# Loading A through casting DMAs from GpSimd, straight into the transposes' input

One Trainium2 chip, one core. The metric is the device time of the kernel in microseconds (us), the median of several executions; all compared runs are in the fast state, with a mean granted TensorE clock of 0.98 to 1.00 of full speed. A profiled execution's span is some 2 us shorter than its time.

## The reference

```python
# a: 4096 x 4096 float32, b: 4096 x 4096 float32, alpha: 0.01
x = np.matmul(a, b)
return np.where(x > 0, x, alpha * x)
```

## The kernel before

The product runs in bf16: 8192 matmuls of 128x128 weights by 512 columns. The output is cut into **regions** of 512 rows by 1024 columns, eight PSUM banks each; a region takes four steps over k (`u`), 1024 deep each, the first one split in two. Two regions that follow each other (h = 0, 1) use the same 1024 columns of B. TensorE needs A transposed: each 128-row block is loaded as fp32 in four DMAs, each of which puts a quarter of the columns on 32 partitions; DVE (in the start for h = 1, ACT) casts it to bf16, and DVE's 32x32 block transpose then leaves k on the partitions.

```python
subs = [(0, 0, 4, 0), (0, 4, 4, 512)] + [(u, 0, 8, 1024 * u) for u in range(1, KU)]
at_pool = ...tile_pool(name="at", bufs=HALVES * KU)
bt_pool = ...tile_pool(name="bt", bufs=KU + 2)
a32_pool = ...tile_pool(name="a32", bufs=4)
a16_pool = ...tile_pool(name="a16", bufs=2)
b32_pool = ...tile_pool(name="b32", bufs=4)
o_pool = ...tile_pool(name="oo", bufs=2)
# ... cut

def load_a(mb, h, sub, mt, scalar=False):
    u, c0, kc, k0 = sub
    # ... cut: allocate at[mb, h, u]
    row = ((mb * HALVES + h) * MT + mt) * P
    w = 32 * kc
    a32 = a32_pool.tile([P, 4, w], FP32, name="a32")
    for q in range(4):
        src = a[row:row + P, k0 + q * w:k0 + (q + 1) * w]
        nc.sync.dma_start(a32[32 * q:32 * q + 32], src.rearrange("(g i) w -> i g w", i=32))
    a16 = a16_pool.tile([P, 4, kc, 32], BF16, name="a16")
    a32_v = a32.rearrange("p g (j c) -> p g c j", c=kc)
    if scalar:
        nc.scalar.copy(a16, a32_v)
    else:
        nc.vector.tensor_copy(a16, a32_v)
    dst = at[mb, h, u][:, c0:c0 + kc, mt * P:(mt + 1) * P]
    nc.vector.transpose(dst.rearrange("p c (g i) -> p g c i", g=4), a16)

def load_b(pi, n, sub, c, scalar=False):
    # ... cut: allocate bt[pi, u]
    b32 = b32_pool.tile([P, RN], FP32, name="b32")
    src = b[k0:k0 + kc * P, n * RN:(n + 1) * RN].rearrange("(p c) n -> p c n", c=kc)
    nc.sync.dma_start(b32, src[:, c, :])
    # ... cut: cast to bt on ACT (start) or DVE

# the first two regions; `ahead` emits the loads of the next step
elif last:                                  # last step of a region
    for mt in range(MT):
        for c in range(kc):
            go(mt, c)                       # matmuls of row block mt
        spill(mt)                           # activation, then
                                            # nc.gpsimd.dma_start(place(0, h, ...), o)
        ahead(mt)
```

SP, GpSimd and the others each work off their instructions in the order in which the program emits them, so what an engine issues waits for everything emitted earlier on that engine (GpSimd's timeline under the result shows it: an output at 97.65 us, one at 101.10, and only then the next loads, at 101.99).

## Time and profile before

| | before |
|---|---|
| time, first rounds | 1837.36 us (1833.26 to 1838.29) |
| matmul time at full pace | 8192 x 0.2158 = 1768 us |
| end of region 0 | 113.4 us |
| PE's waits in the first 135 us | 45 us, of which 35 before 92 us |
| DMA, 8 to 60 us | 268 GB/s at share 1.02 |

1768 us is what TensorE needs with every operand at hand, so the question is only what the first two regions lose. The end of region 0 is read from the timeline of ACT: the activation of its last row block starts when the last matmul of that block is done. In this line (start, duration, group, idle time before it) that is at 113.44 us.

```profile
113.44 1.09 ACT L237 ACTIVATE o<-ps 128x512 f32<-128x512 f32 x2 [1.37 <-PE ps L106]
```

In the profile PE is TensorE, PEld its weight load, DVE VectorE, ACT ScalarE, POOL GpSimd and SP SyncE; what follows "<-" in brackets ended an engine's wait. The lines for all this are in the prediction; two more are needed for later: the windows view of the stage with loads of both A and B (columns: PE, weight load, DVE, ACT, POOL busy with counts, granted clock, DMA share, GB/s), and the page's line on the chain that ended last.

```profile
8.00:60.00 52.00, 30.31 (x105) 11.40 (x107) 20.93 (x24) 16.74 (x16) 0.00 (x0) 0.74 1.02 268
```

```profile
PE ps L106 93%; DMA b<-in_b_dram 4%; DMA a<-in_a_dram 1%; SPq L82 0%; ACT bt L101 0%; ACT a L86 0%; DVE at L90 0%; ACT o L294 0%; SPq L99 0%; ACT o L237 0%; ACTq L86 0%; ACTq L237 0%
```

Where packet times are quoted, they are means of the trace's packet records by queue and size. When a part of A or B "had started" is read from the same records, on the clock of the views (the first packet of the load queue is at 1.75 to 1.77 us in every run). The recorded expectations have such times 1 to 2 us later, as they were set by the last packet of each run.

The record of a packet holds the bytes written. A packet of a casting DMA writes half of what it reads, so in the GB/s and KB of the views below A counts half wherever a DMA casts. I say "read" where I have put it at its full size.

### The profile page before, as it was taken

Reading aid. Unit: us, or ns where it says so; the run is one execution under the profiler, and the core shown is the slowest. Engines: PE = TensorE matmul, PEld = TensorE weight load, DVE = VectorE, ACT = ScalarE, POOL = GpSimd, SP = SyncE. Lnnn points to the kernel's source line nnn. Section 1 sums busy time; section 2 is a strip of 40 time slices with the busy share of each in tenths; the row PEclk is TensorE's granted clock in tenths of the full one; section 3 lists DMA queues with packets and bytes.
Section 4 is the critical chain, followed back from the end, with each engine's and each line's share of the span. In section 5 each row is a group of like instructions: output and inputs, shape, how many; then the busy total and the mean of one; then the engine's idle time right before and its main releaser. Section 6 shows DMA issues by size and latency. Waiting matters only on the chain.

```text
span 1834.5 us, 19653 instructions
## 1 busy us (share of the span) xinstructions
PE 1777.4 (97%) x8041; PEld 804.5 (44%) x8204; DVE 536.0 (29%) x685; ACT 207.0 (11%) x310; POOL 73.3 (4%) x128
## 2 busy tenths in 40 slices
PE   5679999999999999999999999999999999999999
PEld 1234444444444444444444444444444444444444
DVE  3434431127642203023661311202665130311000
ACT  3363000000000000000000000000000000000001
POOL 0000000000000000000000000000000000000000
PEclk7889999999999999999999999999999999999999
DMA  9989975338765718254684734716678281644111
GB/s 249 268 218 302 364 274 205 138 128 214 195 243 192 267 57 329 97 186 132 183 259 180 262 152 172 287 46 212 161 188 307 115 337 58 233 180 153 77 46 47
DMA packets 171163, 353.67 MB, mean 193 GB/s; under 512 B 19008, under 2 KB 100928, under 8 KB 171072
## 3 DMA queue, kind: packets, MB, share of 16 engines
q1 hardware_dynamic: 153216, 287.38, 49.3%
q0 software_dynamic: 17856, 65.02, 9.0%
q8 instruction: 64, 1.05, 0.2%
q14 instruction: 27, 0.22, 0.0%
HBM read 285.21 MB, written 67.11 MB: 192 GB/s over the span
## 4 chain that ended last, share of the span: by engine, by line
PE 93%; DMA 5%; ACT 1%; issue 1%; SPq 0%; DVE 0%; ACTq 0%
PE ps L106 93%; DMA b<-in_b_dram 4%; DMA a<-in_a_dram 1%; SPq L82 0%; ACT bt L101 0%; ACT a L86 0%; DVE at L90 0%; ACT o L294 0%; SPq L99 0%; ACT o L237 0%; ACTq L86 0%; ACTq L237 0%
## 5 line engine op out<-in xcount | busy, mean ns | idle before, releaser
L106 PE MATMUL ps<-bt,at 128*128 128x512 bf16 x8029 | 1772.9, 381 | 51.2 <-DVE at L90 29.6
L106 PEld LDWEIGHTS <-at 128*128 128x128 bf16 x8192 | 803.0, 98 | 1021.1 <-DVE at L90 35.2
L103 DVE CAST bt<-b 128x1024 bf16<-128x1024 f32 x384 | 256.9, 692 | 876.1 <-PE ps L106 575.3
L294 ACT ACTIVATE o<-ps 128x512 f32<-128x512 f32 x240 | 130.7, 595 | 1524.5 <-PE ps L106 1386.7
L90 DVE STREAM_TRANSPOSE at<-a 128x1024 bf16<-128x1024 bf16 (+1 forms) x160 | 165.1, 1032 | 218.3 <-PE ps L106 141.4
L88 DVE CAST a<-a 128x1024 bf16<-128x1024 f32 (+1 forms) x140 | 122.2, 873 | 70.8 <-DMA a<-in_a_dram 70.8
L298 POOL DMA_DIRECT2D out_dram<-o x116 | 68.2, 588 | 1531.8 <-ACT o L294 1526.3
L101 ACT CAST bt<-b 128x1024 bf16<-128x1024 f32 x32 | 33.5, 1046 | 64.8 <-DMA b<-in_b_dram 64.8
L86 ACT CAST a<-a 128x1024 bf16<-128x1024 f32 (+1 forms) x20 | 33.1, 1673 | 19.8 <-DMA a<-in_a_dram 19.7
L238 POOL DMA_DIRECT2D out_dram<-o x8 | 4.9, 608 | 172.1 <-ACT o L237 172.1
L237 ACT ACTIVATE o<-ps 128x512 f32<-128x512 f32 x16 | 8.7, 597 | 14.7 <-PE ps L106 8.9
L131 PE MATMUL ps<-w 128*128 128x512 bf16 x12 | 4.4, 548 | 2.3 <-ACT w L128 2.3
L131 PEld LDWEIGHTS <-w 128*128 128x128 bf16 x12 | 1.5, 133 | 4.7 <-ACT w L128 2.3
L128 ACT ACT_TABLE_LOAD x1 | 1.3, 1283 | 0.7 <-PEq L316 0.7
L127 DVE MEMSET w<- 128x256 uint32 x1 | 0.3, 272 | 0.9 <-PEq L316 0.9
L128 ACT ACTIVATE w<-w 128x8 bf16<-128x8 bf16 x1 | 0.2, 210 | 0.0
L316 POOL MEMSET const-float32-0.0<- 128x1 f32 x1 | 0.1, 99 | 0.2 <-issue 0.2
L316 POOL MEMSET const-bfloat16-1.0<- 128x1 bf16 x1 | 0.1, 103 | 0.0
L316 POOL MEMSET const-float32-1.0<- 128x1 f32 x1 | 0.1, 99 | 0.0
L316 POOL MEMSET const-uint8-127<- 128x1 uint8 x1 | 0.1, 99 | 0.0
## 6 DMA issues: line engine op xcount, KB each, us to landing
b<-in_b_dram SPq DMA_DIRECT2D x416, 512.0 KB, 5.5
out_dram<-o POOLq DMA_DIRECT2D x124, 512.0 KB, 3.4
a<-in_a_dram SPq DMA_DIRECT2D x384, 128.0 KB, 4.4
a<-in_a_dram SPq DMA_DIRECT2D x256, 64.0 KB, 2.3
out_dram<-o SPq DMA_DIRECT2D x8, 256.0 KB, 2.0
```

Of the source, the lines that this page charges most:

```text
L86: nc.scalar.copy(a16, a32_v)
L88: nc.vector.tensor_copy(a16, a32_v)
L90: nc.vector.transpose(dst.rearrange("p c (g i) -> p g c i", g=4), a16)
L101: nc.scalar.copy(bt[pi, u][:, c0 + c, :], b32)
L103: nc.vector.tensor_copy(bt[pi, u][:, c0 + c, :], b32)
L106: nc.tensor.matmul(ps, at[mb, h, u][:, c, mt * P:(mt + 1) * P], bt[pi, u][:, c, nt * NT:(nt + 1) * NT], start=first, stop=last,)
L128: nc.scalar.activation(w[:, :8], w[:, :8], LRELU, alpha=alpha)
L131: nc.tensor.matmul(wp, w[:, :P], w, start=True, stop=True)
L237: nc.scalar.activation(o[:, nt * NT:(nt + 1) * NT], done, LRELU, alpha=alpha)
L238: nc.gpsimd.dma_start(place(0, h, pairs[0], mt), o)
L294: nc.scalar.activation(o[:, cols], banks[mt, nt], LRELU, alpha=alpha)
L298: nc.gpsimd.dma_start(to, o)
```

## The change

The intent is to let the DMA do the cast: fp32 in HBM is rounded to bf16 on the way into the transposes' input. That removes one pass of DVE or ACT over A, its fp32 buffers, and most of what SP issues in the start. Such DMAs are issued by GpSimd. Two row blocks are taken per load, so most transposes have 2048 elements a partition (1024 in the first step), and they read with the stride, in elements, that the cast had before.

```diff
-    a32_pool = ctx.enter_context(tc.tile_pool(name="a32", bufs=4))
-    a16_pool = ctx.enter_context(tc.tile_pool(name="a16", bufs=2))
+    a16_pool = ctx.enter_context(tc.tile_pool(name="a16", bufs=4))
...
-        row = ((mb * HALVES + h) * MT + mt) * P
+        row = (mb * HALVES + h) * RM + 2 * mp * P
         w = 32 * kc
-        a32 = a32_pool.tile([P, 4, w], FP32, name="a32")
+        a16 = a16_pool.tile([P, 8, w], BF16, name="a16")
         for q in range(4):
-            src = a[row:row + P, k0 + q * w:k0 + (q + 1) * w]
-            nc.sync.dma_start(a32[32 * q:32 * q + 32], src.rearrange("(g i) w -> i g w", i=32))
-        a16 = a16_pool.tile([P, 4, kc, 32], BF16, name="a16")
-        a32_v = a32.rearrange("p g (j c) -> p g c j", c=kc)
-        if scalar:
-            nc.scalar.copy(a16, a32_v)
-        else:
-            nc.vector.tensor_copy(a16, a32_v)
-        dst = at[mb, h, u][:, c0:c0 + kc, mt * P:(mt + 1) * P]
-        nc.vector.transpose(dst.rearrange("p c (g i) -> p g c i", g=4), a16)
+            src = a[row:row + 2 * P, k0 + q * w:k0 + (q + 1) * w]
+            nc.gpsimd.dma_start(a16[32 * q:32 * q + 32], src.rearrange("(g i) w -> i g w", i=32))
+        dst = at[mb, h, u][:, c0:c0 + kc, 2 * mp * P:2 * (mp + 1) * P]
+        nc.vector.transpose(
+            dst.rearrange("p c (g i) -> p g c i", g=8), a16.rearrange("p g (j c) -> p g c j", c=kc)
+        )
```

Cut: the loops that call `load_a` count pairs of row blocks (`mp`) in place of `mt`, the interleaving of A and B loads is adapted ("abbabb", "abbbabbbbb"), and the first step's matmuls go by pairs of row blocks.

More of the change, by code (lines that the diff above doesn't have):

```diff
@@ L70, with load_a @@
     bt = {}
-    def load_a(mb, h, sub, mt, scalar=False):
+    def load_a(mb, h, sub, mp):
         u, c0, kc, k0 = sub
@@ L159 @@
                 pieces = [
-                    lambda mb=mb, h=h, sub=sub, mt=mt: load_a(mb, h, sub, mt)
+                    lambda mb=mb, h=h, sub=sub, mp=mp: load_a(mb, h, sub, mp)
                     for sub in subs_of[u]
-                    for mt in range(MT)
+                    for mp in range(MT // 2)
                 ]
@@ L182, in step_loads @@
         if h:
-            return [lambda mt=mt: load_a(0, 1, sub, mt, True) for mt in range(MT)]
-        order = "abababab" if sub[2] == 4 else "ababbabbabbb"
+            return [lambda mp=mp: load_a(0, 1, sub, mp) for mp in range(MT // 2)]
+        order = "abbabb" if sub[2] == 4 else "abbbabbbbb"
         made, na, nb = [], 0, 0
@@ L187, in step_loads @@
             if what == "a":
-                made.append(lambda mt=na: load_a(0, 0, sub, mt))
+                made.append(lambda mp=na: load_a(0, 0, sub, mp))
                 na += 1
@@ L245 @@
         if i == 0:
-            for c in range(kc):
-                for mt in range(c):
-                    go(mt, c)
-                for cc in range(c + 1):
-                    go(c, cc)
+            for mts, cs in (((0, 1), (0, 1)), ((2, 3), (0, 1)), ((0, 1, 2, 3), (2, 3))):
+                for c in cs:
+                    for mt in mts:
+                        go(mt, c)
             for quarter in range(4):
```

## The prediction

> **What bounds the kernel now.** I read the page first: busy times, then the 40 slices.
>
> ```profile
> span 1834.5 us, 19653 instructions
> PE 1777.4 (97%) x8041; PEld 804.5 (44%) x8204; DVE 536.0 (29%) x685; ACT 207.0 (11%) x310; POOL 73.3 (4%) x128
> ...
> PE   5679999999999999999999999999999999999999
> ...
> PEclk7889999999999999999999999999999999999999
> ```
>
> PE is full in all slices but the first three (a slice is 45.9 us), and so is its clock. In the chain of work that ended last, 49 matmuls take 10.74 us and the next such piece starts 10.79 to 10.80 us later, 50 matmuls with the one between: 0.216 us each. The product needs 8192 of them, 8192 x 0.216 = 1768 us. So about 66 us of the 1834 are not matmul time, and only those can be won. The waits of PE over the whole run and after 100 us say where they lie:
>
> ```profile
> PE ps L106 <- DVE at L90: 29.6, 10, 5.6
> PE ps L106 <- ACT bt L101: 12.9, 8, 3.1
> ```
>
> ```profile
> PE ps L106 <- DVE at L90: 4.0, 3, 1.6
> PE ps L106 <- ACT bt L101: 0.4, 1, 0.4
> ```
>
> Columns: microseconds in total, times, longest. After 100 us PE waits 4.4 us in all; its last wait ends at 133 us. The rest is start. From then on PE is the bound, and nothing that DVE, ACT or the DMAs save there can shorten the run. The start is two regions: region 0 (rows 0 to 511 by the first 1024 columns of B, 256 matmuls, 55 us at full pace) ends at about 113 us; region 1 (the next 512 rows, same B) follows. What holds region 0 is seen in the windows view (PE time, granted clock, DMA share, GB/s), and in what ended the engines' idle time between 8 and 100 us:
>
> ```profile
> 8.00:100.00 92.00, 54.76 (x202) 21.39 (x206) 0.78 1.00 264
> 100.00:113.00 13.00, 12.52 (x49) 5.15 (x49) 0.82 0.59 184
> 123.00:135.00 12.00, 9.46 (x44) 4.00 (x43) 1.00 1.07 231
> 200.00:229.00 29.00, 28.84 (x133) 13.11 (x135) 1.00 0.98 359
> ```
>
> ```profile
> ACT bt L101 <- DMA b<-in_b_dram: 60.2, 31, 4.6
> DVE a L88 <- DMA a<-in_a_dram: 54.1, 19, 5.4
> ```
>
> Both casting engines wait for transfers, and the DMA engines are at share 1.00 for 92 us. **The start is bound by DMA throughput**, at only 264 GB/s, while the same engines move 359 GB/s at the same share from 200 to 229 us, where only B and some output move. The packets of A are what is slow. Averaging the trace's packet records by size: a 4 KB packet (B) has a median of 159 ns where A is absent and a mean of 219 ns from 8 to 100 us; a 1 KB packet of A has a tenth percentile of 46 ns and a mean of 73 ns there; a 512-byte packet of A, median 27 and mean 34 ns.
>
> **What the Trainium skill says.** (1) "SBUF — State Buffer", Door 1: The DMA port swizzle: the rate into SBUF depends on how many of 16 ports the partitions reach, 27 GB/s each ("DMA: Bandwidth & Descriptors", Specifications, for the rate per engine), and 32 adjacent partitions reach 8. Every DMA of A goes to 32 partitions. Two engines on one port have 13.6 GB/s each, so 1024 bytes need an estimated 75 ns; the mean of 73 against the fastest 46 agrees. (2) "DMA: Bandwidth & Descriptors", SWDGE vs HWDGE vs iDMA: a cast in a DMA is possible only from GpSimd, whose cores write each descriptor. The trace before has GpSimd issue output DMAs of 128 packets, 0.59 us each. Nothing casts in a DMA there, and no page I found states the rate of a casting packet. (3) "SBUF — State Buffer", the "DVE blocks DMA" trap: VectorE in a two-port mode keeps GpSimd from writing descriptors. In the start VectorE would only transpose, at 1245 ns for 1024 elements, no fast mode, so I expect no such stall there; later its B casts (692 ns for 1024, faster than one element a cycle) could each delay a DMA of A by 0.7 us, against a lead of seven slots of 13.8 us (64 matmuls each).
>
> **The change, part by part.**
>
> ```profile
> L88 DVE CAST a<-a 128x1024 bf16<-128x1024 f32 (+1 forms) x140 | 122.2, 873 | 70.8 <-DMA a<-in_a_dram 70.8
> L86 ACT CAST a<-a 128x1024 bf16<-128x1024 f32 (+1 forms) x20 | 33.1, 1673 | 19.8 <-DMA a<-in_a_dram 19.7
> L298 POOL DMA_DIRECT2D out_dram<-o x116 | 68.2, 588 | 1531.8 <-ACT o L294 1526.3
> ```
>
> Removed: 140 DVE casts (122 us) and 20 ACT casts (33 us). DVE is busy 29% and PE-bound stages do not feel it; of these only the latency in the start counts. 160 transposes become 80 of twice the size: from 711 ns for 512 and 1245 for 1024 elements the slope is 1.04 ns an element, so 2.31 us for 2048. The strided side moves from the cast to the transpose; the cast ran one element a cycle with it (1058 ns for 1024), so I charge nothing. Removed from SP: 640 issues of about 0.4 us. SP was not the main bound.
>
> Added on GpSimd: 320 DMAs of 256 packets. From 0.53 to 0.59 us for 128 packets I estimate 1.1 us each, 4.4 us for a tile of 256 rows. The 40 DMAs of region 0 need 44 us, less than their transfer stage, so generation is not the bound there. The first tile comes at about 0.7 + 4.4 + 2 (landing, as the small DMAs before), transpose 1.25: first matmul at 8.4 us, against 7.94 before. No gain, no loss.
>
> **Transfers in region 0.** HBM bytes stay the same, 8.4 MB of A and 16.8 MB of B; packets too: 4096 of 512 B, 6144 of 1 KB, 4096 of 4 KB. But A writes half the bytes into the half-reached ports. If casting is free, an engine's share of a port now carries 512 bytes in 38 ns, less than the 46 ns of the fastest packet, so the read side sets 46 (27 for the small) and B is stretched less, say 170 ns. Over 16 engines: A 4096 x 27/16 = 6.9 us and 6144 x 46/16 = 17.7; B 4096 x 170/16 = 43.5; sum 68 us, with a start of 3 us done at 71. Before: last B tile on hand near 99.5. Then comes what came before too: the last step runs rows outermost, 64 matmuls = 13.8 us, so region 0 ends near 85 instead of 113. **Gain 28 us.**
>
> **Order on GpSimd, given back.** Loads of region 1's A stood on SP, which ran ahead (they begin at 93 us). On GpSimd they stand behind region 0's output DMAs, which wait for PE. In program order the first tile of region 1 follows the output of row block 1, the second that of row block 3, thus after region 0's last matmul. With T that end: output at T+2, generation until T+6.5, landing T+8.5, transpose T+9.8. The first step of region 1 needs all four row blocks in its first quarter, so PE idles about 9 us; the next two steps each need two more tiles of 4.4 us generation against 6.9 us of matmuls, some 2 to 3 us more each. About 14 us instead of 4: **loss 10 us.** By region 2 the queue is ahead: GpSimd needs 44 us for region 1's A, PE 55 us. In later row blocks the same order costs nothing, by the seven-slot lead. B for region 2 (16.8 MB) now need not queue on SP behind A, but still waits for buffers.
>
> Sum with free casting: 1837 - 28 + 10 = 1819 us.
>
> **Rivals.** *The port story is wrong or casting costs about what it saves* (1 KB packet near 73 ns, B near 219): the transfer stage stays, the loss on GpSimd's order stays: 1837 + 8 to 10 = 1846. For: rows of A lie 16 KB apart, and the slow mean could be HBM's; against: the 46 and 73 ns pair fits two engines to a port. *Casting packets are slow* (an estimate for the case: 150 ns for 1 KB, 75 for 512 B): A in region 0 takes 6144 x 150/16 + 4096 x 75/16 = 77 us, with B at 170 a stage of 120; region 0 ends near 137, region 1 is fed at 77 us against 55 of matmuls: 24 + 20 to 30 slower, 1880 to 1890. Nothing in the profile speaks for or against, since no DMA here casts. *GpSimd becomes the bound* (2 us and more per DMA): region 0 takes 80 us of generation, region 1 as much against 55 us of matmuls; gain gone, 1845 to 1865. Against: 0.53 us for 128 packets. *All hidden:* after 135 us PE is full whatever happens; this holds for 1700 us of the run and is why every outcome but the slow packet stays within 2%.
>
> **Range and chances.** 2% is 37 us. Faster than 1800 needs more than half of the 66 us; even pure B rate (25.2 MB at 415 GB/s, the best slices of the stretch from 135 to 229 us, is 61 us) with no loss of order only just gets there: 0.06. Slower than 1874 needs packets over about 130 ns or generation over 2.5 us: 0.13. The rest, 0.81, is the same within 2%. I weigh free casting about 0.55, the equal case 0.2, slow packets or slow GpSimd 0.25. Point 1822 us, range 1804 to 1868.
>
> **What would show it.** Right: region 0 ends at 80 to 90 us, the rate from 8 us to there is above 320 GB/s, 1 KB packets have a mean near 46 to 50 ns and B's falls towards 170; PE's waits put 8 to 10 us on the transpose at the start of region 1, released by a DMA that GpSimd issued after region 0's last output; DVE falls by about 130 us without effect; matmuls after 150 us still come every 0.216 us. Wrong: packets of the software queue above 100 ns, GpSimd instructions above 1.5 us each, VectorE waiting on A throughout region 1, or any PE wait after region 2 begins, which would mean that the seven-slot lead does not cover output DMAs ahead of loads.

## The result

The changed kernel took 1827.97 us (1827.43 to 1828.4, 4 runs), the kernel before 1837.82 us in the same rounds (1833.26 to 1842.58). The ratio is 0.9946, 95% interval 0.992 to 0.9971. Here and below a ratio is the mean time of one kernel's fast runs over that of the other's of the same rounds, so not quite the ratio of the quoted medians. The gain is real and half a per cent: the same within 2%, and inside the predicted range. The kernel before scatters more than the changed ones and moved between 1834 and 1839 us from one set of rounds to another, so each ratio is to the kernel before in the same rounds. The changed kernel itself ran in the first rounds only: what is said of a few microseconds between it and the experiments compares different rounds, and how far the changed kernels move from one set to another was not measured.

The page after, busy times and the groups that changed (busy us, mean ns, then idle time before them):

```profile
span 1825.7 us, 18868 instructions
...
PE 1776.4 (97%) x8041; PEld 804.5 (44%) x8204; DVE 475.6 (26%) x465; ACT 174.3 (10%) x290; POOL 253.6 (14%) x448
...
PE ps L101 93%; DMA a<-in_a_dram 4%; POOL a L81 0%; POOL out_dram L233 0%; DVE at L83 0%; ACT o L288 0%; DVEq L83 0%; POOLq L81 0%; POOLq L233 0%; POOLq L310 0%
...
L83 DVE STREAM_TRANSPOSE at<-a 128x2048 bf16<-128x2048 bf16 (+1 forms) x80 | 219.4, 2779 | 365.1 <-DMA a<-in_a_dram 241.9
...
L81 POOL DMA_DIRECT2D a<-in_a_dram x320 | 183.4, 587 | 83.4 <-DMA a<-in_a_dram 50.5
```

All casts of A are gone, yet DVE's total fell by only 60 us: the transposes now take 219 us, not 165. In the chain that ended last, 4% of the span moved from B's transfers to A's. The windows view for the two stages that matter, and PE's waits after 100 us:

```profile
8.00:60.00 52.00, 27.60 (x80) 9.83 (x82) 12.61 (x6) 30.03 (x29) 15.47 (x27) 0.67 1.18 340
60.00:100.00 40.00, 37.92 (x172) 16.96 (x174) 15.34 (x5) 4.58 (x8) 6.87 (x12) 1.00 0.58 128
100.00:120.00 20.00, 12.77 (x51) 5.36 (x53) 8.66 (x6) 0.80 (x2) 16.51 (x29) 0.83 1.07 141
```

```profile
PE ps L101 <- DVE at L83: 7.3, 2, 6.1
```

From 8 to 60 us the DMAs moved 340 GB/s in place of 268. In bytes read it is more: the casting queue, q0, wrote 2.51 MB in these 52 us and so read twice as much, which makes 388 GB/s. But PE did less in that stage, 27.60 us in place of 30.31, and from 60 to 100 us it was nearly full (37.92 of 40) while the DMAs were half idle. The timelines of PE and of ACT say how:

```profile
43.42 1.89 PE L101 MATMUL ps<-bt,at 128*128 128x512 bf16 x4 [3.90 <-DVE at L83]
54.50 16.70 PE L101 MATMUL ps<-bt,at 128*128 128x512 bf16 x63 [9.20 <-DVE at L83]
72.91 26.94 PE L101 MATMUL ps<-bt,at 128*128 128x512 bf16 x121 [1.71 <-DVE at L83]
101.05 1.04 PE L101 MATMUL ps<-bt,at 128*128 128x512 bf16 x4 [1.20 <-DVE at L83]
108.22 112.13 PE L101 MATMUL ps<-bt,at 128*128 128x512 bf16 x501 [6.13 <-DVE at L83]
```

```profile
99.72 1.09 ACT L232 ACTIVATE o<-ps 128x512 f32<-128x512 f32 x2 [2.36 <-PE ps L101]
```

Region 0 ends at 99.7 us, 13.7 us earlier than before. PE lies still until 54.5 us for the second tile of step u = 1. Then, at the border to region 1, it waits 1.20 + 6.13 us. What it waits for in the first case is told by the DMA view for 8 to 60 us (packets, MB and share of the engines of the casting queue; then size written and median us from issue to landing), and by the waits of GpSimd up to 100 us (us in total, times, longest):

```profile
q0 software_dynamic: 7203, 2.51, 40.6%
...
b<-in_b_dram SPq DMA_DIRECT2D x29, 512.0 KB, 6.0
a<-in_a_dram POOLq DMA_DIRECT2D x19, 128.0 KB, 19.7
```

```profile
POOL a L81 <- DMA a<-in_a_dram: 45.3, 24, 2.9
```

A casting DMA of 256 packets took 19.7 us to land, while a DMA of B, with twice the bytes to read, took 6.0. By the packet records B's 16.8 MB had started to the last packet at 59 us, but only half of A's 8.4 MB at 50 us. GpSimd had eight loads in flight at most, in this kernel and in all the others that load A from it, and before 100 us it waited 45.3 us for one to land before it issued the next; whether that number comes from the chip or from the software is not shown. In the second case it is the order on GpSimd, seen in the timeline of POOL:

```profile
97.65 0.56 POOL L233 DMA_DIRECT2D out_dram<-o  x1 [0.64 <-ACT o L232]
101.10 0.55 POOL L233 DMA_DIRECT2D out_dram<-o  x1 [2.88 <-ACT o L232]
101.99 7.99 POOL L81 DMA_DIRECT2D a<-in_a_dram  x14 [0.35 <-issue]
```

The second A tile of region 1 is issued after region 0's last output.

So there were four things to test: whether the transfer rate rose because half the bytes go to the half-reached ports; whether A was late because B's queue took the engines' time; whether the order on GpSimd cost what it seems to; and what the slow transposes cost.

### The profile page after: what moved, and what is told of

Same layout as the page of the kernel before. It is cut to its first block, busy times and chain, and to the rows that moved or that the text cites. A ratio compares the mean times of both kernels' runs of the same rounds, so it can differ in the third digit from the quotient of the medians.

```text
span 1825.7 us, 18868 instructions
## 1 busy us (share of the span) xinstructions
PE 1776.4 (97%) x8041; PEld 804.5 (44%) x8204; DVE 475.6 (26%) x465; ACT 174.3 (10%) x290; POOL 253.6 (14%) x448
## 4 chain that ended last, share of the span: by engine, by line
PE 93%; DMA 4%; issue 2%; POOL 1%; DVE 0%; ACT 0%; POOLq 0%; DVEq 0%
PE ps L101 93%; DMA a<-in_a_dram 4%; POOL a L81 0%; POOL out_dram L233 0%; DVE at L83 0%; ACT o L288 0%; DVEq L83 0%; POOLq L81 0%; POOLq L233 0%; POOLq L310 0%
## 5 line engine op out<-in xcount | busy, mean ns | idle before, releaser
L83 DVE STREAM_TRANSPOSE at<-a 128x2048 bf16<-128x2048 bf16 (+1 forms) x80 | 219.4, 2779 | 365.1 <-DMA a<-in_a_dram 241.9
L81 POOL DMA_DIRECT2D a<-in_a_dram x320 | 183.4, 587 | 83.4 <-DMA a<-in_a_dram 50.5
```

The lines of the kernel that those rows point to most:

```text
L81: nc.gpsimd.dma_start(a16[32 * q:32 * q + 32], src.rearrange("(g i) w -> i g w", i=32))
```

## The experiments

Ten kernels ran, in three sets.

### Region 0's outputs from SP

```diff
-                nc.gpsimd.dma_start(place(0, h, pairs[0], mt), o)
+                (nc.gpsimd if h else nc.sync).dma_start(place(0, h, pairs[0], mt), o)
```

> Changed kernel, with the four output DMAs of region 0 issued by SP, so that region 1's loads of A no longer stand behind them on GpSimd. Theory (order on GpSimd costs time at the start of region 1): PE's waits after 100 us fall from 7.3 us to under 2, the loads of region 1's A are issued before 85 us, and the time falls from 1828 by 6 to 8 us, to 1820 to 1822. Rival (those waits come from transfer or transpose, not from the order): PE still waits 5 us or more there, time within 2 us of 1828.

Measured: 1818.17 us (1817.68 to 1819.74), ratio to before 0.9906. After 98 us PE has no wait left at all. The timelines of PE and of POOL:

```profile
55.31 164.91 PE L101 MATMUL ps<-bt,at 128*128 128x512 bf16 x750 [10.89 <-DVE at L83]
```

```profile
61.82 4.75 POOL L81 DMA_DIRECT2D a<-in_a_dram  x8 [1.59 <-DMA a<-in_a_dram]
```

PE's matmuls run on from 55.31 us without a gap over the border, and GpSimd goes straight on to region 1's A from about 62 us. The mechanism is shown. The gain is 9.8 us between the medians of different rounds, 9.7 us between the profiled spans, and 7.3 us by the two ratios to the kernel before, so it is likely, but not certain, that it exceeds the 7.3 us of waits. Part of what is over would be that the matmuls after such a wait run at a lower clock: from 100 to 120 us the changed kernel's granted clock was 0.83, here 1.00.

### B in packets of half the size

```diff
-        nc.sync.dma_start(b32, src[:, c, :])
+        if pi == 0:
+            for s in range(2):
+                nc.sync.dma_start(b32[:, s * NT:(s + 1) * NT], src[:, c, s * NT:(s + 1) * NT])
+        else:
+            nc.sync.dma_start(b32, src[:, c, :])
```

> Changed kernel, with region 0's B tiles loaded in two DMAs of 2 KB rows in place of one of 4 KB rows. Theory (the DMA engines take packets of the two queues in turn, so the packet size sets the shares; with 1 KB of A against 4 KB of B, A comes too late): A's read rate in the mixed stage rises from about 95 to about 120 GB/s or more, about one packet of A per packet of B still, the last transpose of region 0 comes earlier, region 0 ends at 92 to 96 us in place of 99.9, time 1821 to 1825. Rival (A is held back by how many DMAs GpSimd may have in flight or by the cast itself): A's rate stays near 95, time 1828 or more, as B gets more packets.

Measured: 1824.96 us, ratio 0.9941. Nothing about A was changed, and yet its read rate, from 8 us to the last packet of B, rose from 97 to 119 GB/s, and half of it had started at 43 us in place of 50. Region 0 ended at 96.4 us by ACT's timeline, at the edge of what was expected. So what B puts into its queue has a hand in how fast A comes, and it is not GpSimd's issue or the cast alone. The total rate fell from 340 to 308 GB/s (388 to 366 read), as more, smaller packets carry B (95 ns for 2 KB against 172 for 4 KB), which may eat a part of the gain. "A packet each in turn", if a record is such a packet, is too simple: in the changed kernel some 1.3 packets of A went by for each of B with 1 KB reads, and 2.6 with 512-byte reads; here 1.0 and 1.3. The exact rule is open. The rival, a limit on GpSimd's loads in flight, exists (eight), but is not what set A's rate: in the last experiment eight loads of half the size brought 92 GB/s read from 8 to 60 us, where the changed kernel's eight brought 97.

### The same loads from GpSimd without the cast

```diff
 # kernel before
-            nc.sync.dma_start(a32[32 * q:32 * q + 32], ...)
+            nc.gpsimd.dma_start(a32[32 * q:32 * q + 32], ...)
```

> Kernel before, with its A loads issued by GpSimd as they are, fp32 without a cast, casts left on DVE and ACT. Theory (the gain of transfer comes from writing half the bytes into the half-reached ports, so only the casting DMA has it): 1 KB packets of A keep a mean of 70 ns or more and B's one above 200, 250 to 280 GB/s in the stage with both, region 0 ends at 108 us or later, time 1838 to 1848 with the order loss on GpSimd. Rival (the gain comes from a second queue or from GpSimd as issuer): A near 50 ns, above 340 GB/s, region 0 ends near 100, time 1826 to 1832.

Measured: 1849.18 us, ratio 1.0071 (1.0047 to 1.0095), the slower side of before. The windows view:

```profile
8.00:60.00 52.00, 27.83 (x83) 9.23 (x84) 22.27 (x26) 19.20 (x19) 31.68 (x53) 0.67 1.04 283
```

The rate from 8 to 60 us was 283 GB/s, a little over the range I gave, and the last group of region 0's matmuls ended at 92.34 + 11.38 = 103.7 us, earlier than I gave. PE then waited 20.7 us after 98 us, because here four smaller loads stand behind the outputs, with casts and transposes behind them. The packet test could not be read as planned: without a cast the trace records A's packets as 4 KB ones, so it seems that four rows of 1 KB went as one. They took 237 ns beside B's 235, 59 ns for each KB against 75 from SP. So a second queue and larger packets together bring something (268 to 283 GB/s), and the cast brings the larger part (to 388 read). The wide spread of B's packets (tenth to ninetieth percentile 168 to 302 ns) stays here, and is gone with the cast (172 to 172).

### The transposes read contiguously

The result is wrong on purpose.

```diff
-            ..., a16.rearrange("p g (j c) -> p g c j", c=kc)
+            ..., a16.rearrange("p g (c j) -> p g c j", c=kc)
```

> Changed kernel, with the transposes reading their bf16 input contiguously in place of with a stride; the result is wrong on purpose. Theory (the stride of 16 bytes slows the read): the 2048-element transpose falls from 3.8 to about 2.3 us, the 1024-element one (stride 8 bytes) stays at 1.25; as region 0 has a few transposes right before PE, time falls by 1 to 4 us. Rival (the transpose's length or its output is what is slow): stays at 3.8 us, time unchanged.

The groups by shape, of the changed kernel and of this one:

```profile
L83 DVE STREAM_TRANSPOSE at<-a 128x2048 bf16<-128x2048 bf16 x48 | 181.6, 3819 | 212.0 <-DMA a<-in_a_dram 184.4 <-PE ps L101 27.6
L83 DVE STREAM_TRANSPOSE at<-a 128x1024 bf16<-128x1024 bf16 x32 | 37.9, 1218 | 153.1 <-PE ps L101 63.7 <-DMA a<-in_a_dram 57.5 <-remote 31.9
```

```profile
L83 DVE STREAM_TRANSPOSE at<-a 128x2048 bf16<-128x2048 bf16 x48 | 110.3, 2307 | 256.1 <-DMA a<-in_a_dram 221.5 <-PE ps L101 34.6
...
L83 DVE STREAM_TRANSPOSE at<-a 128x1024 bf16<-128x1024 bf16 x32 | 38.6, 1229 | 162.1 <-PE ps L101 95.5 <-DMA a<-in_a_dram 66.4
```

The stride of 16 bytes costs 1.5 us per transpose of 2048 elements; the stride of 8 bytes costs nothing. Length is not what is slow: in the last experiment a transpose of 1024 elements with the stride of 16 bytes took 2.01 us, where the same size with 8 bytes takes 1.22. The time, 1826.57 us over 7 runs (1825.73 to 1831.9), is 1.4 us below the changed kernel's of another set of rounds, and both profiled spans are 1825.7 us: 71 us less work on DVE is worth next to nothing.

### Both edits

> Changed kernel with both edits: region 0's outputs issued by SP and region 0's B in 2 KB packets. Theory: the two gains lie in different places (start of region 1; share of A in region 0) and add: 1818 - 3 = 1815 us, 1813 to 1817, PE's waits after 98 us zero and A's second half landed before 46 us. Rival (the second gain is lost once GpSimd runs ahead, because region 1's A then takes the engines from B): 1817 to 1820.

Measured: 1815.82 us, ratio 0.9883. It has the region 1 edit of the first experiment and the packet edit of the second. Half of A had started at 43 us, PE had no wait after 98 us: the two gains add about as expected, 2.3 us below the first edit alone (in other rounds).

### The kernel before, writing A to all partitions

Each DMA reads the same rows from HBM in packets of the same size, and the DMAs come in the same order; the partitions that a DMA writes to are others, so the result is wrong on purpose. Not quite the same is, by the access patterns, the order of the rows within a DMA: 0, 1, 2, ... in place of 0, 32, 64, 96, 1, ...

```diff
 # kernel before
-            nc.sync.dma_start(a32[32 * q:32 * q + 32], src.rearrange("(g i) w -> i g w", i=32))
+            nc.sync.dma_start(a32[:, q, :], src)
```

> Kernel before, with the same reads of A from HBM (128 rows of 1 KB or 512 B per DMA, fp32, SP), but each DMA written to all 128 partitions in place of 32; the result is wrong on purpose. Theory (the 32-partition destination, which reaches half the ports, is what makes A's packets and B's beside them slow): 1 KB packets fall from a mean of 73 to about 46 to 52 ns, B's from 219 to 160 to 180, the rate from 8 to 60 us rises from 264 to 330 GB/s or more, region 0 ends at 85 to 95 us, time 1808 to 1820, without any cast in a DMA. Rival (HBM's row pitch or the packet size is what is slow): 70 to 75 ns, time within 5 us of the kernel before.

Measured: 1814.32 us, ratio 0.9872. Windows view:

```profile
8.00:60.00 52.00, 35.60 (x136) 13.78 (x136) 27.05 (x29) 22.62 (x22) 0.00 (x0) 0.84 0.99 340
```

The DMA share is 0.99 and the rate 340 GB/s where the kernel before had 268; from 8 to 58 us a 1 KB packet of A fell from 75 to 48.5 ns and B's from 222 to 181; region 0 ended at 90.5 us by ACT's timeline, where it had been 113.4. No cast was moved and no queue added, and the packet size, which is the same here, is not the cause. One rival this run leaves: the other order of rows within a DMA. Two other runs answer it. The kernel of the last experiment and the one with GpSimd's plain loads read the same rows in the same old order, from the same queue, 128 rows a load, and write the same 32 partitions; with the cast they read 392 GB/s from 8 to 60 us and B's packets took 168 ns, without it 283 GB/s and 235 ns (the buffers and the recorded size of A's packets differ too). So the bytes that go to 32 partitions are what made A slow in the kernel before, and B beside it: more partitions mend it, and half the bytes mend it. And this kernel gains more than twice as much time as the change (1.28% against 0.54%), though it reads less from 8 to 60 us (340 GB/s against 388): A and B come through one queue in the order of need, and region 1's loads do not stand behind outputs.

### Fewer buffers for B

Both on top of the first experiment:

```diff
-    b32_pool = ctx.enter_context(tc.tile_pool(name="b32", bufs=4))
+    b32_pool = ctx.enter_context(tc.tile_pool(name="b32", bufs=2))   # and 3 in the other
```

> As e1_outs_sp (region 0's outputs from SP), with 2 buffers for B's fp32 tiles in place of 4. Theory (B's queue takes turns with A's whenever it is not empty, so B arrives long before PE can use it and A is late): with B's queue empty part of the time, A's second half lands before 45 us in place of 51.8; if B stays ahead of need the time falls to 1813 to 1817. Against it: B may become the late one[...]; then PE waits for ACT's casts of B and the time is 1820 or more.

> As e1_outs_sp, with 3 buffers for B's fp32 tiles. Theory: between e1_outs_sp and e7_b2bufs in A's arrival; A's second half lands at 47 to 51 us, time 1815 to 1818. Rival (depth of B's queue does not matter so long as it is never empty): A as in e1_outs_sp, 51.8 us, time 1817 to 1820.

Measured with two: 1841.27 us, ratio 1.0024. A came early (half started at 25 us), and B became the late one: it moved at 138 GB/s from 8 to 60 us, its last packet started only at 108 us, and PE waited for ACT's casts of it:

```profile
PE ps L101 <- ACT bt L96: 42.2, 25, 2.7
```

Measured with three: 1813.31 us (1812.49 to 1815.44), ratio 0.987, lower than expected. The windows and DMA views for 8 to 60 us:

```profile
8.00:60.00 52.00, 43.81 (x169) 18.03 (x170) 26.09 (x10) 22.46 (x22) 22.91 (x41) 0.84 1.26 304
```

```profile
b<-in_b_dram SPq DMA_DIRECT2D x22, 512.0 KB, 6.0
a<-in_a_dram POOLq DMA_DIRECT2D x24, 128.0 KB, 11.5
```

With one buffer less for B, A's DMAs land in 11.5 us in place of the changed kernel's 19.7, half of A has started at 30 us in place of the first experiment's 50, and PE gets 43.81 us of matmuls into that stage in place of its 25.88. The bytes read are as many (385 GB/s against 388). Depth of B's queue does matter; the rival falls. Together with the second experiment this shows that the split between the two queues, and not the total rate, held region 0.

### Three buffers and a gate

```diff
-                nc.gpsimd.dma_start(place(0, h, pairs[0], mt), o)
+                (nc.sync if h == 0 and mt else nc.gpsimd).dma_start(place(0, h, pairs[0], mt), o)
```

with `bufs=3` for B.

> Changed kernel with 3 buffers for B's fp32 tiles and region 0's outputs 1 to 3 issued by SP, output 0 left on GpSimd as a gate: region 1's A then starts when PE has finished the first row block of region 0, after B has landed, and not behind the last output. Theory: in e8_b3bufs PE's last waits of region 0 (67 to 80 us) come from region 1's A taking packets from B, so here B lands by 72 us in place of 79.8, region 0 ends 4 us or more earlier, region 1 starts with a wait under 2 us; time 1808 to 1812, below e8's 1813.3. Rival (B is late in e8 for want of a third buffer's depth alone): B lands at 77 us or later, and the gate only adds a wait: 1813 or more.

Measured: 1813.19 us (1813.01 to 1813.33), ratio 0.9866: no better than without the gate. The last packet of B had started at 71.5 us in place of 78.4, and the last of region 0's eight activations started at 85.9 us in place of 94.3, as the theory has it; but region 1's A, now held back by the gate, came late, and PE waited 5.7 us for it. These microseconds were moved, not won. The two versions with three buffers beat the kernel before by 1.3%, and the changed kernel by some 0.8%, across rounds; both are under 2%.

### The cast without the merging of row blocks

The changed kernel with 640 casting DMAs of 128 packets, one row block each, the matmul order of the kernel before and 8 buffers.

```diff
-    def load_a(mb, h, sub, mp):                 # 2 row blocks, [P, 8, w]
+    def load_a(mb, h, sub, mt, scalar=False):   # 1 row block,  [P, 4, w]
-    a16_pool = ...(name="a16", bufs=4)
+    a16_pool = ...(name="a16", bufs=8)
```

> Changed kernel with loads of 128 rows in place of 256 (640 casting DMAs of 128 packets), the matmul order of the kernel before and 8 buffers: the cast alone, without the merging of row blocks. Theory: the first tile lands after half as many packets, first matmul at 8 to 10 us in place of 12.2; the shares of A and B per packet stay, so A's half still lands at 49 to 53 us; the wait at the start of region 1 becomes shorter, 3 to 5 us, as the last tile is half as large; time 1822 to 1828. Rival (per-DMA cost on GpSimd matters): region 0 is held by GpSimd, time 1830 or more.

Measured: 1832.48 us over 20 runs, ratio 0.9963 (0.9954 to 0.9972): a miss, 4.5 us above the changed kernel by the medians of different rounds, though the intervals of the two ratios touch. The first matmul came at 10.85 us, the waits after 98 us were 8.7 us, not 3 to 5, and half of A had started at 52 us. GpSimd was busy for 45 of the 92 us from 8 to 100, so its time for issuing is not what held this kernel. About 0.56 us per DMA is what GpSimd spent here with 128 packets, and 0.59 in the changed kernel with 256. Why A is still a little later than with merged loads (92 against 97 GB/s read) was not separated; eight loads in flight of half the size would fit.

## Why the prediction was right or wrong

**The bound was right.** After region 1's start nothing changed: PE has no wait after the one that ends at 108.2 us, and 60 us less DVE work and 33 us less ACT work bought nothing there. The run stayed within 2%.

**The rate was right, and its reason is shown.** Over 320 GB/s were predicted, with A counted as read; 388 were measured from 8 to 60 us, and B's packet, predicted at 170 ns, took 171. Writing A to all partitions, alone, raised the rate too, to 340. A casting packet took 59 and 41 ns, where 46 and 27 were assumed, the fastest plain ones. But its time is not what it costs an engine, since such packets overlap. From 68 to 72 us A alone was being moved:

```profile
68.00:72.00 4.00, 3.20 (x15) 1.27 (x13) 2.95 (x1) 0.00 (x0) 1.22 (x3) 1.00 1.45 193
```

The share is 1.45, and 1509 packets of 1 KB read started, which over 16 engines is one each 42 ns on an engine, less than the 46 assumed (for the 512-byte reads this was not worked out). The sum of the transfers was nearly right as well: all was to be done at 71 us, and the last packet of A started at 74.

**The step that failed is the one after it**: "Then comes what came before too: the last step runs rows outermost, 64 matmuls = 13.8 us, so region 0 ends near 85 instead of 113. Gain 28 us." The measured end was 99.7, the gain 13.7 us. That sentence took it that only the last of four steps is left when the transfers end, which holds if A and B still arrive in the order of need, as they did in SP's one queue. In two queues they did not: the last packets of B had started at 59 us and of A at 74, and PE could begin the second of the four steps in earnest only at 54.5 us. Three quarters of region 0's matmuls, 188 or 41 us, were still to do then, which with a last wait of 1.7 us and some 3 us for matmuls at the lower clock makes 99.7; at 72.91 us, near the end of the transfers, there were still 121 recorded ones to do, not 64. The experiments that changed only B's queue moved the time at which half of A had started from 50 us to 43, and, on top of the first experiment, from 50 to 30. None of the prediction's four rivals has the two queues' shares in it; "GpSimd becomes the bound" was the nearest, and it was not the cause.

**The order on GpSimd was right in kind**, with the place, the wait and its releaser, and too large in size: 10 us of loss were predicted. The waits grew from 4.0 to 7.3 us: of the 9 us at the border most came true, and the 2 to 3 us at each of the next two steps did not come at all. Everything after region 0's end took 4.9 us more (1825.7 - 99.7 = 1726.0 against 1834.5 - 113.4 = 1721.1); the other 1.6 us are in keeping with the lower clock after the wait. The main reason is that a DMA of 256 packets took GpSimd 0.59 us and not 1.1: the estimate scaled with packets, and the time goes with the DMA (0.56 with 128). Issuing the outputs elsewhere won 7 to 10 us. The stall of GpSimd beside VectorE's casts, the third point from the skill, was not put to the test: none of the 320 loads was issued during a cast of B, and the longest took 0.73 us. The two terms as measured, -13.7 + 4.9, give the measured difference of the spans, -8.8 us; -28 + 10 was predicted. Both terms were about twice too large, in opposite directions, so the sum was so too. That 1822 came within 6 us of 1828 is in part luck, two errors that partly cancel, and in part that both terms are small beside the 1768 us of matmuls.

**Transposes**: 2.31 us were predicted, 3.82 measured; contiguous reads gave 2.31. "I charge nothing" for the stride was wrong, and its reason was a misreading: the strided cast's 1058 ns were taken as free of cost, but in the trace before the contiguous cast of B, of the same shape and types, took VectorE 692 ns; on ScalarE it was 2047 against 1046. It cost little, as DVE is not the bound. **First matmul**: 8.4 us predicted, 12.2 measured; the first tile's DMAs shared the engines with B's first four tiles, which fits the same cause but was not tested on its own.

## What to carry to other kernels

When loads move to another queue, ask not only for the total rate but in which order the data of the two queues arrives: one queue kept the order that was written here, two shared by what was in them, and the depth and packet size of the one changed the pace of the other. An engine's queue also keeps program order, so loads put on the engine that issues outputs stand behind outputs; put one of the two elsewhere. And when a DMA writes to a quarter of the partitions, look at its packets' spread before blaming HBM: here fewer bytes and more partitions each mended it.

## What the Trainium skill lacked or had wrong

- "DMA: Bandwidth & Descriptors" gives no rate for a casting DMA. Here a packet that read 1 KB and wrote 512 bytes took 59 ns and one of 512 bytes 41 ns, against 46 and 27 of the fastest plain ones from SP (different queue, so the cast is not the only difference). They overlapped: with A alone on the engines, one each 42 ns on an engine.
- The same page, in "Issuing engines are not separate DMA queues", says that DMAs of several issuers interleave on the same engines and that issuing from several saves only sequencer time. The order of arrival changes as well: A's DMAs landed in 19.7 us beside B's in 6.0, and in 11.5 us with one buffer less for B, worth about 5 us of the run. Its section "Queues, rings and completion order" names turns by packet; 1.3 or 2.6 recorded packets of A passed for each of B in the changed kernel, 1.0 or 1.3 with B's packets halved. Whether a record is a packet in the page's sense no run shows.
- No page says that casting DMAs are recorded row by row, with the bytes written as their size (512 bytes for 1 KB read), where the same plain DMAs from GpSimd are recorded in packets of 4 KB (237 ns).
- No page found says how many loads GpSimd has in flight: never more than eight here, of 128 or of 256 packets.
- "SBUF — State Buffer", Door 1: The DMA port swizzle, is borne out: 75 ns and 268 GB/s with 32 partitions a DMA, 48.5 ns and 340 GB/s with 128. The summary's "Prefer 32 over 64" holds no warning that B's DMAs beside it suffer too (222 against 181 ns).
- The same page's note on 16-byte lines (each access to a new line pays) fits the bf16 transpose: 3.82 us at a stride of 16 bytes, 2.31 contiguous, no cost at 8 bytes. The fp32 casts of the kernel before were slower with a stride of 32 bytes too, against contiguous ones of another tensor: 1058 against 692 ns for 1024 elements on VectorE, 2047 against 1046 on ScalarE. No run changed their stride alone.
- No page gives GpSimd's time per DMA by packets: 0.56 us with 128 packets, 0.59 with 256.
